# A two-layer streaming encoder step: where the MLP products' operands lie modulo 64 bytes, where sample combinations and first splits are kept, and another order in the MLP's opening

## The chip, the core and the metric

One core of a Trainium2 chip runs the whole step as one program. The metric is the device time of one execution in microseconds (us), median of several. Of the core's engines TensorE (PE) multiplies matrices, VectorE (DVE) and ScalarE (ACT) work elementwise, GpSimd (POOL) adds a little and issues some DMA, and SyncE (SP) issues most DMA.

## The reference

Two layers over a prompt of 1024 rows and 8 x 16 = 128 sample rows of width 1024. Layer 0 mixes by stick-breaking attention and a convolution module, layer 1 by banded attention. Both have the same MLP, which is what the change touches:

```
for layer in range(2):
    ...                                   # mixer and its output projection
    xp = xp + sq_relu_mlp(rmsnorm(xp, norm_ffn[layer]), w_up[layer], w_down[layer])
    xs = xs + sq_relu_mlp(rmsnorm(xs, norm_ffn[layer]), w_up[layer], w_down[layer])

def sq_relu_mlp(h, w_up, w_down):         # w_up 1024 x 4096, w_down 4096 x 1024, float32
    return jnp.square(jax.nn.relu(h @ w_up)) @ w_down
```

## The kernel before

**Products.** Each float32 operand is split in a rounded high part and a low remainder, and a product of two operands is three products on TensorE (high x high, high x low, low x high: `SPLIT`). The function `split` makes the high part on ScalarE (L186) and the low one on VectorE (L187). Both MLP matrices are multiplied in blocks by a scheme of seven products in place of eight (as Strassen's), so that sums of blocks of the activations and of the weights are made first.

**`rest(layer, ...)`** does, for one layer, the second half of the output projection (PSUM tiles `psob`), then the MLP's up stage, then its down stage. Its tiles in SBUF come from a pool under a name each (`own`: xr, xr2, xr3, hl0, hl1, th, tm, sm, lo0 to lo2, t1, sl0 to sl11); tiles named b11m, t2m, rwm, wm, wkm, hdm and the like come from another pool (`place`); weights in flight from a third (`sp`, names st for raw ones, hl_m and hl_wd for split ones). Pools are laid out one behind another in the order of first use.

**Up stage.** The blocks of the normed activations are `b11, b21, b22` and the sums `t1` to `t4`, each in four slices c, made by `combine` between the last products of the output projection (`evac`). `homes_of` and `where` say which tile each one lies in: t1, b21 and t3 of slice 2 are tiles lo0, lo1 and lo2, slices 0 and 1 are tiles sl. `units(u)`, u from 0 to 7, makes the hidden rows of one eighth of w_up: for k from 0 to 6 and two halves e, `seven(i, e)` with i = 7u + k prepares split weights, `mms` issues 12 products of 128 x 512 into `um` (L1604; moving operand: activations, stationary: weights) and `take` collects. The 128 sample rows take part by `sample(k)`, after products 0, 2, 3 and 6: its products `usm` (L1616) have the sample columns of a combination as stationary operand and the weights as moving one. A row `um<-t2m,hl_m` reads moving operand, then stationary. Those columns lie in the 128 last places (`NS`) of the tile of some combination, and `sample_combo` says of which. In unit 0 four pairs (k, e) are issued first over three slices (`early`), while the norms of the rows are still being finished (`ms_m`, `v_m`, by `rstd_of`).

**Down stage.** Products `pd` (L1889; activations moving, weights stationary) and, for the samples, `ps` (L1909; weights moving). `load_b` loads hidden blocks from HBM into the halves of xr, `split_b` splits them into four tiles in turn; `load_w` and `resident` load raw weights (a22 into lo0, lo1, lo2, xr3, sl8 to sl11, two blocks a tile; others into st), `weights_hi` makes their high part into hl_wd, hl0 or hl1 (L1830), `weights_lo` the low one (L1836). `run_at(i)` issues what is planned ahead of product i; `begin` issues the first two steps of it inside the last unit (u = 7) of the up stage.

**Order.** A scheduler orders each engine's instructions by expected times and by who waits for whom; what passes through `pinned` keeps the order in which it is written, and a tile is written anew only when all that read its last content are done.

Of the kernel before, what the change touches and what calls it, by code (L numbers as in the profile page):

```python
# [15 lines left out]
P = 128  # L16
# [108 lines left out]
def tile_trunk(ctx, tc, ins, outs):  # L125
# [132 lines left out]
    def rstd_of(r, pl, acc, scale, eps, name, pin=lambda ins: ins, cnt=NG):  # L258

        tp = P
        ms = bank(f"ms_{name}")
        for j in range(cnt):
            ins = mm(ms[:tp, j:j + 1], acc[:, j * tp:(j + 1) * tp], ones[:, 0:1], start=True, stop=True)
            if j == 0:
                pin(ins)
        v = pl.tile([P, 2, 4], F32, tag="rv", name=f"v_{name}")
# [1073 lines left out]
    def rest(layer, ks, cat, rst, mp, then, soon=None):  # L1342
# [12 lines left out]
        def pair(t, n=1024):  # L1355

            return t[:, :n].rearrange("p (a t) -> p a t", a=2)
# [29 lines left out]

        def sample_combo(key, c):

            return [home(k, c)[:, NS] for k in {"s1": ("b11", "t2"), "s2": ("b21", "b22"), "sd": ("t1", "t3")}[key]]  # L1390


        wo = ins["w_out_ab"] if layer == 0 else ins["w_out_c"]
# [50 lines left out]
        def evac(n, ps, g):  # L1444
            fc = order[n]
            xs = x[fc][:, g * G:g * G + G]
            tt(xs, xs, ps[:, :G], ALU.add)
            nx.square(xs, fc, slice(g * G, g * G + G), n == 0, add=nc.gpsimd.tensor_tensor)
            if g == NG - 1:
                put(xr_d[layer][fc], x[fc])  # L1450
                if n % 2:
                    todo.extend(combine(fc - 4))

                    if n < 7:
                        todo.append((lambda: (old(n + 3), old(n + 4))) if n < 4 else (lambda: whole_raw(0)))
            some(3)
            if n == KC - 1 and g == 1:
                seven(0, 0)


        raws, ups = {}, {}
# [27 lines left out]
        def seven(i, e):  # L1489
# [2 lines left out]
            m = 2 * u + e  # L1492
            if (i, e) in ups or m >= NF // 2:
                return
            a11, a12, a21, a22 = (raws[m, r][:, h * 512:h * 512 + 512] for r in range(2) for h in range(2))
            if k == 0:
                src = a11
            elif k == 1:
                if ("s1", m) not in ups:
                    two_sums(m)  # L1500
# [92 lines left out]
        def units(u):  # L1593
# [68 lines left out]
            start = 0  # L1662
            if u == 0:

                early = ((0, 0), (1, 0), (2, 0), (0, 1))
                for n, (k, e) in enumerate(early):
                    mms(k, e, range(3))
                    if n == 0:
                        seven(2, 0)
                    elif n == 1:  # L1670
                        seven(0, 1)
                    some(4)
                some(99)
                nx.end(0, pin=pinned)
# [115 lines left out]
        def split_b(i):  # L1790
            while len(bsplit) < 4 and len(bsplit) <= i:
                q = len(bsplit)
                if q < 2:
                    bsplit.append(pair(own(("th", "xr2")[q], F32R)))
# [412 lines left out]
```

## Time and profile before

| | us |
|---|---|
| median of 3 runs (lowest, highest) | 2742.29 (2740.29, 2743.49) |
| the profiled execution's own time | 2734.41 |
| its span in the trace | 2732.6 |
| up stage of layer 0, from first um to first pd | 577.00 to 956.46 |
| up stage of layer 1 | 1981.16 to 2354.97 |

All times in the profile are from the one profiled execution, counted from the span's start; 1.8 us lie around the span. A row of the timeline reads: start, length, engine, line, operation, out<-in by the program's names with buffer numbers left out (the second input of a product is the stationary one), partitions x elements, and how many instructions follow one another in it; in brackets, how long the engine stood idle before it and whose result ended that. Windows give the engines' busy time in a stretch, then the mean granted TensorE clock (1.00 is full), the busy share of the DMA engines and their rate.

### The profile page before, as it was taken

How to read it: one execution, taken by the hardware profiler on the slowest of the kernel's cores; microseconds unless marked ns; L12 is line 12 of the kernel's file. 1: busy time of each engine (PE TensorE's matmuls, PEld its weight loads, DVE VectorE, ACT ScalarE, POOL GpSimd, SP SyncE). 2: the span in 40 equal slices, each digit the busy share in tenths (PEclk: the TensorE clock that was granted, in tenths of full speed). 3: DMA queues.
4: the chain of work that ended last, by engine and by line, in shares of the span. 5: the costliest groups of instructions: out<-in, count | busy, mean ns of one | idle time of the engine just before them, and what ended most of it. 6: DMA issues, size and time to landing. Idle time of an engine off the chain costs nothing.

```text
span 2732.6 us, 42141 instructions
## 1 busy us (share of the span) xinstructions
PE 2672.6 (98%) x15404; PEld 2317.0 (85%) x15404; DVE 1988.5 (73%) x3820; ACT 1342.6 (49%) x2691; POOL 314.8 (12%) x535
## 2 busy tenths in 40 slices
PE   8999999999999999999999999999999999999998
PEld 8898877888888778888999999989978888788888
DVE  8999987886766644767577777778886767546677
ACT  6344457754444443445355555556554544433444
POOL 1000110121111100000011111110311111000001
PEclk9999999999999999999999999999999999999999
DMA  4444556533444387435544444446533434685344
GB/s 158 117 122 146 155 169 217 185 104 142 147 151 145 130 311 245 143 115 179 158 139 138 141 138 136 140 149 221 182 129 139 151 143 146 244 274 167 98 145 141
DMA packets 193807, 437.04 MB, mean 160 GB/s; under 512 B 26960, under 2 KB 71184, under 8 KB 191552
## 3 DMA queue, kind: packets, MB, share of 16 engines
q1 hardware_dynamic: 154032, 297.69, 33.5%
q0 software_dynamic: 39424, 136.64, 14.3%
q8 instruction: 121, 1.98, 0.3%
q14 instruction: 86, 0.70, 0.1%
q10 hardware_dynamic: 144, 0.02, 0.0%
HBM read 299.03 MB, written 122.58 MB: 154 GB/s over the span
## 4 chain that ended last, share of the span: by engine, by line
PE 83%; DVE 9%; ACT 3%; DMA 3%; issue 2%; POOL 0%; SPq 0%; DVEq 0%; ACTq 0%; POOLq 0%
PE um L1604 22%; PE psc L226 10%; PE psp L226 4%; PE usm L1616 3%; PE ps L1909 3%; PE psoa L226 2%; PE avc L488 2%; PE tpc L476 2%; PE f L226 1%; PE pd100None L1889 1%; PE pd000None L1889 1%; PE pd001None L1889 1%; PE pd101None L1889 1%; PE pd002None L1889 1%; PE pd102None L1889 1%
## 5 line engine op out<-in xcount | busy, mean ns | idle before, releaser
L226 PE MATMUL psc<-h,hl_wc 128*128 128x384 f32 x1728 | 329.1, 340 | 0.0
L226 PEld LDWEIGHTS psc<-h,hl_wc 128*128 128x128 f32 x1728 | 296.9, 188 | 9.2 <-issue 7.9
L1604 PE MATMUL um<-sl,hl_m 128*128 128x512 f32 x780 | 201.9, 398 | 0.0
L756 DVE SCALAR_TENSOR_TENSOR y<-u,dw,y 128x1024 f32<-128x1024 f32 (+1 forms) x232 | 177.4, 805 | 0.7
L1604 PEld LDWEIGHTS um<-sl,hl_m 128*128 128x128 f32 x780 | 145.2, 188 | 34.3
L226 PE MATMUL psp<-h,hl_wi 128*128 128x384 f32 x864 | 162.4, 340 | 0.0
L226 PEld LDWEIGHTS psp<-h,hl_wi 128*128 128x128 f32 x864 | 148.3, 188 | 6.2 <-issue 5.1
L187 DVE TENSOR_TENSOR tm<-xr,tm 128x512 fp32r<-128x512 f32 (+1 forms) x120 | 78.2, 652 | 101.6 <-ACT tm L186 101.4
L186 ACT ACTIVATE tm<-xr 128x512 fp32r<-128x512 f32 (+1 forms) x120 | 71.9, 599 | 124.0 <-PE pd103None L1889 26.1
L1230 ACT ACTIVATE s<-s,mxc 128x640 f32<-128x640 f32 (+4 forms) x128 | 88.8, 694 | 40.4 <-DVE mxc L1227 38.7
L186 ACT ACTIVATE whc<-tpc 128x512 fp32r<-128x512 f32 (+1 forms) x144 | 72.2, 523 | 63.8 <-PE tpc L476 60.6
L1227 DVE CUSTOM_DVE_ANT_0 s<-zc,bp 128x384 f32<-128x384 f32 (+3 forms) x128 | 66.0, 517 | 41.3 <-PE zc L1264 40.8
L1604 PE MATMUL um<-sl,hl 128*128 128x512 f32 x372 | 94.2, 392 | 0.5 <-DVE hl L187 0.5
L187 DVE TENSOR_TENSOR xr<-xr,xr 128x512 fp32r<-128x512 f32 (+1 forms) x60 | 39.2, 654 | 75.5 <-ACT xr L186 75.2
L187 DVE TENSOR_TENSOR wlc<-tpc,whc 128x512 fp32r<-128x512 f32 (+1 forms) x144 | 83.1, 594 | 7.5 <-ACT whc L186 6.7
L1628 ACT ACTIVATE xr<-xr 128x512 f32<-128x512 f32 x64 | 40.4, 632 | 91.4 <-DVE xr L1627 91.4
L1604 PEld LDWEIGHTS um<-sl,hl 128*128 128x128 f32 x372 | 69.0, 188 | 16.1 <-DVE hl L187 1.4
L1604 PE MATMUL um<-b11m,hl_m 128*128 128x512 f32 x288 | 72.5, 404 | 6.3 <-ACT hl_m L186 5.5
L476 PE MATMUL tpc<-ident,s 128*128 128x128 f32 x480 | 73.5, 276 | 3.6 <-DVE s L1232 3.0
L187 DVE TENSOR_TENSOR th<-xr,th 128x512 fp32r<-128x512 f32 (+1 forms) x62 | 40.6, 655 | 49.3 <-ACT th L186 49.3
L186 ACT ACTIVATE hl_m<-xr 128x512 fp32r<-128x512 f32 x54 | 34.1, 631 | 78.4 <-PE usm L1616 64.4
L1604 PEld LDWEIGHTS um<-b11m,hl_m 128*128 128x128 f32 x288 | 54.8, 195 | 18.8 <-ACT hl_m L186 6.4
(1055 smaller groups left out, 7150.8 us busy)
## 6 DMA issues: line engine op xcount, KB each, us to landing
xr<-hb_d SPq DMA_DIRECT2D x208, 256.0 KB, 2.8
xr<-in_w_up_dram SPq DMA_DIRECT2D x32, 512.0 KB, 3.8
rwm<-in_w_up_dram SPq DMA_DIRECT2D x32, 512.0 KB, 4.8
hb_d<-xr POOLq DMA_DIRECT2D x32, 512.0 KB, 3.3
hb_d<-t POOLq DMA_DIRECT2D x32, 512.0 KB, 3.2
wm<-in_w_down_dram SPq DMA_DIRECT2D x64, 256.0 KB, 3.5
st_wd<-in_w_down_dram SPq DMA_DIRECT2D x64, 256.0 KB, 3.5
st_wc<-in_w_in_c_dram SPq DMA_DIRECT2D x44, 256.0 KB, 2.9
```

Source lines behind the costliest of these rows:

```text
L186: ACT(hi, src, AF.Copy)
L187: return tt(lo, src, f(hi), ALU.subtract)
L226: mm(ps()[:, :G], hl[:, a, at:at + P], act[g][k // 4][b][:, k % 4, :], start=n == 0, stop=n == len(todo) - 1)
L476: nc.tensor.transpose(tp[:, c0 + q * P:c0 + (q + 1) * P], blocks.get(j, tile_q), ident)
L488: mm(st["av"][:, o0:o0 + n], vs[:, j, i].rearrange("p a d -> p (a d)"), src[:, c0:c0 + n], start=st["done"] == 0, stop=st["done"] == nmm - 1)
L756: stt(src if j == CW - 1 else dst, src, wj, dst, ALU.mult, ALU.add)
L1227: nc.vector.tensor_tensor_reduce(s[:, c:c + m], z, b, -1.0, mx, ALU.add, ALU.min, new)
L1230: ACT(s[:, :n], s[:, :n], AF.Exp, bias=mx, scale=-1.0, accum_out=tot)
L1604: mm(banks[b, e], w[a][:, c], combo(key, c)[:, h], start=k < 3 and c == 0 and i == 0, stop=c == 3 and i == 2, skip_group_check=k > 2)
L1616: mm(samples[u][:, e * 256:e * 256 + 256], sample_combo(key, c)[h], w[a][:, c].rearrange("p e t -> p (e t)"), start=k == 0 and c == 0 and ...
L1889: mm(ps, w[:, a, m * P:m * P + P], b[:, h], start=first and s == 0, stop=j == NJ - 1 and s == 2, skip_group_check=k not in heads)
L1909: mm(rows[e], s[:, h], w[:, a], start=j == 0 and q == 0 and k != 0, stop=j == NJ - 1 and q == 2 and k != 3, skip_group_check=k in (3, 0))
```

## The change

Five edits, the kernel otherwise as before:

1. In `rstd_of` the tile v is [P, 2, 8] in place of [P, 2, 4], 64 bytes a partition in place of 32. What is laid out behind it moves by 32 bytes.
2. `sample_combo`: the sample columns of s1 lie in the tiles of t1 and t2 (before b11 and t2), s2 in b21 and t3 (before b21 and b22), sd in t4 and b22 (before t1 and t3). Sample products k = 0 and 2 use s1, 3 uses s2, 6 uses sd.
3. `split_b`: the first two of the four tiles for split blocks are the halves of tm, the other two th and xr2 (before the other way round).
4. seven(0, 1) is called right behind seven(0, 0), at the end of the output projection; its block a11 comes from a tile st_a11 of its own, by one more load of 256 KB in each layer, in place of raws[1].
5. `early`: (0,0), (0,1), (1,0), (2,0) in place of (0,0), (1,0), (2,0), (0,1).

Two lines are added above the MLP's lines, so L1604 is L1606 after, L1616 is L1618, L1581 is L1583; the down stage's lines keep their numbers.

```
--- before.py
+++ after.py
@@ -265,7 +265,7 @@
             ins = mm(ms[:tp, j:j + 1], acc[:, j * tp:(j + 1) * tp], ones[:, 0:1], start=True, stop=True)
             if j == 0:
                 pin(ins)
-        v = pl.tile([P, 2, 4], F32, tag="rv", name=f"v_{name}")
+        v = pl.tile([P, 2, 8], F32, tag="rv", name=f"v_{name}")
         m, y = v[:, 0, :cnt], v[:, 1, :cnt]
         nc.vector.tensor_scalar(m, ms[:tp, 0:cnt], scale, eps, ALU.mult, ALU.add)
         ACT(y, m, AF.Sqrt)
@@ -1387,7 +1387,7 @@
 
         def sample_combo(key, c):
 
-            return [home(k, c)[:, NS] for k in {"s1": ("b11", "t2"), "s2": ("b21", "b22"), "sd": ("t1", "t3")}[key]]
+            return [home(k, c)[:, NS] for k in {"s1": ("t1", "t2"), "s2": ("b21", "t3"), "sd": ("t4", "b22")}[key]]
 
 
         wo = ins["w_out_ab"] if layer == 0 else ins["w_out_c"]
@@ -1456,6 +1456,7 @@
             some(3)
             if n == KC - 1 and g == 1:
                 seven(0, 0)
+                seven(0, 1)
 
 
         raws, ups = {}, {}
@@ -1492,9 +1493,10 @@
             m = 2 * u + e
             if (i, e) in ups or m >= NF // 2:
                 return
-            a11, a12, a21, a22 = (raws[m, r][:, h * 512:h * 512 + 512] for r in range(2) for h in range(2))
+            if i or not e:
+                a11, a12, a21, a22 = (raws[m, r][:, h * 512:h * 512 + 512] for r in range(2) for h in range(2))
             if k == 0:
-                src = a11
+                src = a11 if i or not e else staging(ins["w_up"][layer, 2][:, :512], f"a11{name}")
             elif k == 1:
                 if ("s1", m) not in ups:
                     two_sums(m)
@@ -1662,13 +1664,11 @@
             start = 0
             if u == 0:
 
-                early = ((0, 0), (1, 0), (2, 0), (0, 1))
+                early = ((0, 0), (0, 1), (1, 0), (2, 0))
                 for n, (k, e) in enumerate(early):
                     mms(k, e, range(3))
                     if n == 0:
                         seven(2, 0)
-                    elif n == 1:
-                        seven(0, 1)
                     some(4)
                 some(99)
                 nx.end(0, pin=pinned)
@@ -1790,8 +1790,8 @@
         def split_b(i):
             while len(bsplit) < 4 and len(bsplit) <= i:
                 q = len(bsplit)
-                if q < 2:
-                    bsplit.append(pair(own(("th", "xr2")[q], F32R)))
+                if q > 1:
+                    bsplit.append(pair(own(("th", "xr2")[q - 2], F32R)))
                 else:
                     bsplit.extend(pair(temp_again()[:, h:h + 1024]) for h in (0, 1024))
             n = bs[i].shape[1]
```

The places of the two operands modulo 64 bytes, by the addresses in the two built programs (moving, stationary; number of products):

| products | before | after |
|---|---|---|
| um L1604, 128 x 512 | (0,0) 468, (32,32) 828, (0,32) 972, (32,0) 420 | (32,32) 2688 |
| pd L1889, 128 x 512 | (0,0) 912, (0,32) 1584 | (32,32) 2496 |
| pd L1889, 128 x 256 | (0,32) 384 | (32,32) 384 |
| ps L1909, 128 x 512 | (0,0) 132, (32,0) 252 | (32,32) 384 |
| usm L1616, 128 x 256 | mixed | (32,32) 768 |
| psob, 128 x 384, of L226 | (32,0) 360, else (32,32) | (32,32) |

Before, the tiles of `own` lie at 0 (xr, xr2, xr3, th, tm, sm, hl0, hl1, lo, sl, t1) and those of `place` and of the stream pool at 32 (b11m, t2m, hl_m, hl_wd, st, rwm, wm, wkm, hdm); after, all lie at 32.

TensorE at the opening of layer 0's up stage; the four digits of um are the layer, u, the bank that a product adds to and e (um0020 collects product 2 of unit 0, e = 0). Before:

```order
L1604 MATMUL um0000_6306<-b11m0_20_6138,hl_m000_6244 128x512 x2
L1604 MATMUL um0000_6306<-b11m0_20_6138,hl_m001_6245 128x512
L1604 MATMUL um0010_6328<-t2m0_01_5842,th0_5634 128x512 x3
L1604 MATMUL um0010_6328<-t2m0_11_6007,th0_5634 128x512 x3
L1604 MATMUL um0010_6328<-t2m0_21_6162,th0_5634 128x512 x3
L1604 MATMUL um0020_6350<-sl00_5645,hl00_5632 128x512 x2
L1604 MATMUL um0020_6350<-sl00_5645,hl10_5633 128x512
L1604 MATMUL um0020_6350<-sl10_5646,hl00_5632 128x512 x2
L1604 MATMUL um0020_6350<-sl10_5646,hl10_5633 128x512
L1604 MATMUL um0020_6350<-lo00_5637,hl00_5632 128x512 x2
L1604 MATMUL um0020_6350<-lo00_5637,hl10_5633 128x512
L1604 MATMUL um0001_6368<-b11m0_00_5808,hl_m000_6244 128x512 x2
```

After:

```order
L1606 MATMUL um0000_6310<-b11m0_20_6138,hl_m000_6244 128x512 x2
L1606 MATMUL um0000_6310<-b11m0_20_6138,hl_m001_6245 128x512
L1606 MATMUL um0001_6332<-b11m0_00_5808,hl_m000_6244 128x512 x2
L1606 MATMUL um0001_6332<-b11m0_00_5808,hl_m001_6245 128x512
L1606 MATMUL um0001_6332<-b11m0_10_5973,hl_m000_6244 128x512 x2
L1606 MATMUL um0001_6332<-b11m0_10_5973,hl_m001_6245 128x512
L1606 MATMUL um0001_6332<-b11m0_20_6138,hl_m000_6244 128x512 x2
L1606 MATMUL um0001_6332<-b11m0_20_6138,hl_m001_6245 128x512
L1606 MATMUL um0010_6352<-t2m0_01_5842,th0_5634 128x512 x3
L1606 MATMUL um0010_6352<-t2m0_11_6007,th0_5634 128x512 x3
L1606 MATMUL um0010_6352<-t2m0_21_6162,th0_5634 128x512 x3
L1606 MATMUL um0020_6370<-sl00_5645,hl00_5632 128x512 x2
```

um0001, the second half of product 0, stands behind um0000 in place of standing behind um0020. Both need only b11m; um0001's weights hl_m000 and hl_m001 are those that seven(0, 1) makes as the other half of the same tiles.

ScalarE around the last sample products of layer 0 (usm07). Before:

```order
L1628 ACTIVATE xr20_5630<-xr20_5630 128x512
L1629 ACTIVATE xr20_5630<-xr20_5630 128x512
L1573 ACTIVATE sl00_9079<-usm07_8770,v_m02_6411 128x512
L186 ACTIVATE th0_9024<-xr0_8964 128x512
L1628 ACTIVATE hdm0_51_6424<-hdm0_51_6424 128x512
L1629 ACTIVATE hdm0_51_6424<-hdm0_51_6424 128x512
L1830 ACTIVATE hl_wd00_9018<-lo00_8968 128x512
L1628 ACTIVATE hdm0_51_6424<-hdm0_51_6424 128x512
L1830 ACTIVATE hl_wd01_9020<-lo00_8968 128x512
L1830 ACTIVATE hl_wd02_9022<-lo10_8971 128x512
L186 ACTIVATE xr20_9027<-xr0_8964 128x512
```

After:

```order
L1630 ACTIVATE xr20_5630<-xr20_5630 128x512
L1631 ACTIVATE xr20_5630<-xr20_5630 128x512
L1830 ACTIVATE hl_wd00_9020<-lo00_8970 128x512
L1830 ACTIVATE hl_wd01_9022<-lo00_8970 128x512
L1830 ACTIVATE hl00_5632<-lo20_9017 128x512
L1630 ACTIVATE xr20_5630<-xr20_5630 128x512
L1631 ACTIVATE xr20_5630<-xr20_5630 128x512
L1830 ACTIVATE hl_wd02_9024<-lo10_8973 128x512
L1575 ACTIVATE sl00_9079<-usm07_8772,v_m02_6413 128x512
L1830 ACTIVATE hl_wd03_9086<-lo10_8973 128x512
L186 ACTIVATE th0_9088<-xr0_8966 128x512
```

The splits of the first down weights (hl_wd00 and hl_wd01 from lo00, hl00 from lo20, hl_wd02 from lo10) stand ahead of sl00<-usm07 in place of behind it; so do the first splits of hidden blocks, tm0, some rows further up, in place of th0<-xr0.

TensorE at the passage from layer 0's up stage to its down stage (pd06m is product 6, bank m). Before:

```order
L1616 MATMUL usm07_8770<-hl_m0551_8926,t1m0_40_6322 128x256
L1889 MATMUL pd060None_9091<-th0_9024,hl_wd00_9018 128x512 x2
L1889 MATMUL pd061None_9095<-th0_9024,hl_wd00_9018 128x512 x2
L1889 MATMUL pd062None_9099<-th0_9024,hl_wd00_9018 128x512 x2
L1889 MATMUL pd063None_9103<-th0_9024,hl_wd00_9018 128x512 x2
L1909 MATMUL ps06_9107<-hl_wd00_9018,sm0_5636 128x512 x2
L1581 MATMUL utm07_9143<-ident_69,sl00_9079 128x128 x4
L1889 MATMUL pd060None_9091<-th0_9024,hl_wd00_9018 128x512
L1889 MATMUL pd061None_9095<-th0_9024,hl_wd00_9018 128x512
L1889 MATMUL pd062None_9099<-th0_9024,hl_wd00_9018 128x512
L1889 MATMUL pd063None_9103<-th0_9024,hl_wd00_9018 128x512
```

After:

```order
L1618 MATMUL usm07_8772<-hl_m0551_8928,t4m0_71_6349 128x256
L1889 MATMUL pd060None_9092<-tm0_8976,hl_wd00_9020 128x512
L1889 MATMUL pd061None_9096<-tm0_8976,hl_wd00_9020 128x512
L1889 MATMUL pd062None_9100<-tm0_8976,hl_wd00_9020 128x512
L1889 MATMUL pd063None_9104<-tm0_8976,hl_wd00_9020 128x512
L1889 MATMUL pd060None_9092<-tm0_8976,hl_wd00_9020 128x512
L1889 MATMUL pd061None_9096<-tm0_8976,hl_wd00_9020 128x512
L1889 MATMUL pd062None_9100<-tm0_8976,hl_wd00_9020 128x512
L1889 MATMUL pd063None_9104<-tm0_8976,hl_wd00_9020 128x512
L1909 MATMUL ps06_9108<-hl_wd00_9020,sm0_5636 128x512
L1889 MATMUL pd060None_9092<-tm0_8976,hl_wd00_9020 128x512
L1889 MATMUL pd061None_9096<-tm0_8976,hl_wd00_9020 128x512
```

The last sample product reads t4m in place of t1m and t3m; the four small transposes utm07 move some ten products back, and the products of the first step read tm0 in place of th0.

SP at the end of the output projection, with the added load. Before, then after:

```order
L1403 DMA xr0_5629<-xm_d0_112 128x1152 x2
L193 DMA st_wo0b6_1_5983<-in_w_out_ab_dram 128x512
L193 DMA st_wo0b7_0_6066<-in_w_out_ab_dram 128x128
L193 DMA st_wo0b7_1_6070<-in_w_out_ab_dram 128x512
L1403 DMA xr20_5630<-xm_d0_112 128x1152
L1403 DMA xr30_5631<-xm_d0_112 128x1152
L1471 DMA xr0_5629<-in_w_up_dram 128x1024 x2
```

```order
L1403 DMA xr0_5629<-xm_d0_112 128x1152 x2
L193 DMA st_wo0b6_1_5983<-in_w_out_ab_dram 128x512
L193 DMA st_wo0b7_0_6066<-in_w_out_ab_dram 128x128
L193 DMA st_wo0b7_1_6070<-in_w_out_ab_dram 128x512
L193 DMA st_a11m0_6248<-in_w_up_dram 128x512
L1403 DMA xr20_5630<-xm_d0_112 128x1152
L1403 DMA xr30_5631<-xm_d0_112 128x1152
L1472 DMA xr0_5629<-in_w_up_dram 128x1024 x2
```

One row is added, st_a11m, behind the last weights of the output projection and ahead of the loads into xr2 and xr3.

More of the change, by code (lines that the diff above doesn't have):

```diff
@@ L267, in rstd_of @@
                 pin(ins)
-        v = pl.tile([P, 2, 4], F32, tag="rv", name=f"v_{name}")
+        v = pl.tile([P, 2, 8], F32, tag="rv", name=f"v_{name}")
         m, y = v[:, 0, :cnt], v[:, 1, :cnt]
@@ L1388, in sample_combo @@
         def sample_combo(key, c):
-            return [home(k, c)[:, NS] for k in {"s1": ("b11", "t2"), "s2": ("b21", "b22"), "sd": ("t1", "t3")}[key]]
+            return [home(k, c)[:, NS] for k in {"s1": ("t1", "t2"), "s2": ("b21", "t3"), "sd": ("t4", "b22")}[key]]
         wo = ins["w_out_ab"] if layer == 0 else ins["w_out_c"]
@@ L1458, in evac @@
                 seven(0, 0)
+                seven(0, 1)
         raws, ups = {}, {}
@@ L1494, in seven @@
                 return
-            a11, a12, a21, a22 = (raws[m, r][:, h * 512:h * 512 + 512] for r in range(2) for h in range(2))
+            if i or not e:
+                a11, a12, a21, a22 = (raws[m, r][:, h * 512:h * 512 + 512] for r in range(2) for h in range(2))
             if k == 0:
-                src = a11
+                src = a11 if i or not e else staging(ins["w_up"][layer, 2][:, :512], f"a11{name}")
             elif k == 1:
@@ L1669, in units @@
                         seven(2, 0)
-                    elif n == 1:
-                        seven(0, 1)
                     some(4)
@@ L1792, in split_b @@
                 q = len(bsplit)
-                if q < 2:
-                    bsplit.append(pair(own(("th", "xr2")[q], F32R)))
+                if q > 1:
+                    bsplit.append(pair(own(("th", "xr2")[q - 2], F32R)))
                 else:
```

2 lines of the change are left out of this document (1 added, 1 removed).

## Prediction

> **What bounds the kernel now.** I read the page's busy shares first, then the chain that ended last, then the work by stretches of the span, then TensorE's rows at the places the change touches.
>
> ```profile
> span 2732.6 us, 42141 instructions
> PE 2672.6 (98%) x15404; PEld 2317.0 (85%) x15404; DVE 1988.5 (73%) x3820; ACT 1342.6 (49%) x2691; POOL 314.8 (12%) x535
> PE 83%; DVE 9%; ACT 3%; DMA 3%; issue 2%; POOL 0%; SPq 0%; DVEq 0%; ACTq 0%; POOLq 0%
> ...
> core 0: us, PE busy (x) PEld busy (x) DVE busy (x) ACT busy (x) POOL busy (x), PEclk, DMA share, GB/s
> 660.00:930.00 270.00, 270.00 (x1321) 226.17 (x1320) 187.29 (x282) 126.49 (x216) 37.21 (x54) 1.00 0.41 146
> 960.00:1320.00 360.00, 358.94 (x1566) 292.08 (x1567) 230.16 (x386) 159.44 (x278) 15.10 (x28) 1.00 0.60 196
> ```
>
> The first row gives the span, the second shows TensorE busy for 98% of it, the third that 83% of the chain that ended last is its products. The last two rows are stretches inside layer 0's up stage and down stage: TensorE is busy for all of 270.00 us and for 358.94 of 360.00, at the full granted clock. There, whatever shortens a product shortens the kernel, and no other engine's work can. What is left to gain otherwise lies in a few places where the products wait: the opening of each up stage and the passage from up to down stage.
>
> **Part 1, the places modulo 64 bytes.** A product's records overlap, so I take the time from the start of one row to the start of the next, over its count. The table of places in the section on the change says which pairs of operands are alike.
>
> ```profile
> 682.04 5.77 PE L1604 MATMUL um<-b11m,hl 128*128 128x512 f32 x24
> 687.65 0.28 PE L1616 MATMUL usm<-hl,b11m 128*128 128x256 f32 x1
> ...
> 727.13 5.61 PE L1604 MATMUL um<-b11m,hl_m 128*128 128x512 f32 x24
> 732.59 0.28 PE L1616 MATMUL usm<-hl_m,b11m 128*128 128x256 f32 x1
> ...
> 734.38 5.72 PE L1604 MATMUL um<-t2m,hl_m 128*128 128x512 f32 x24
> 739.93 1.56 PE L1604 MATMUL um<-sl,hl 128*128 128x512 f32 x6
> ...
> 1133.29 0.86 PE L1889 MATMUL pd000None<-tm,hl_wd 128*128 128x512 f32 x3
> 1138.89 0.86 PE L1889 MATMUL pd000None<-th,hl 128*128 128x512 f32 x3
> ...
> 1140.97 0.84 PE L1889 MATMUL pd003None<-th,hl 128*128 128x512 f32 x3
> 1143.69 0.85 PE L1889 MATMUL pd003None<-xr,hl 128*128 128x512 f32 x3
> ```
>
> In the up stage, b11m with hl (unlike) takes (687.65 - 682.04) / 24 = 233.8 ns a product; b11m with hl_m (alike) 5.46 / 24 = 227.5; t2m with hl_m (alike too) 5.55 / 24 = 231.3. In the down stage eight rows of three from 1133.29 to 1138.89 (tm with hl_wd, unlike) take 5.60 / 24 = 233.3, four rows from 1140.97 to 1143.69 (th and xr with hl, alike) 2.72 / 12 = 226.7. So an unlike pair costs 2.5 to 6.6 ns more, with TensorE always busy and at full clock; the same b11m is fast and slow, so it is the pair and not the tile.
>
> After the change all pairs of the MLPs are alike. By the table, 1392 products of L1604, 1584 of L1889 with 512 columns, and 252 of L1909 stop being unlike. For L1889 I take the 6.6 ns just shown: 1584 x 6.6 ns = 10.5 us. L1909 is the same form with the operands exchanged; at 6.6 ns it is 252 x 6.6 = 1.7 us. For L1604 the alike rows spread from 227.5 to 231.3; with every pair alike I expect 228.5, nearer the low end, because a group with hl_m at 231.3 stands between groups that are unlike and the down stage's alike rows lie at 226.7: 1392 x (234.0 - 228.5) = 7.7 us, with 234.0 the rounded unlike value. Sum 19.9, say 20 us.
>
> Bounds. Low: 2.5 ns for L1604 (3.5 us), 10.5 for L1889, nothing for L1909, 14 us. High: all L1604 products at 227.5, which also speeds up those alike already (1392 x 6.3 = 8.8 us and at most 1296 x 3.8 = 4.9 us), 26 us. For the 768 sample products and the 384 of 256 columns in the down stage I take nothing; the upper bound, half of 6.6 ns for half the columns, would add 1152 x 3.3 ns = 3.8 us. The 32 bytes themselves (v's tile) add no instruction.
>
> A rule speaks against this part. The Trainium skill, "TensorE: Matmul & The Clock Gate", section "Step-by-step: what each phase is for", says that TensorE reads the moving operand and the next weights through two independent ports, so that a weight load takes nothing from the running product. By it the places would be worth nothing; the rows above differ by pair and disagree. I keep what follows from it as rival A.
>
> **Part 2, from up to down stage.** The order's excerpts show it: before, layer 0's first down product waits for hl_wd00, made on ScalarE from lo00, and the load into lo00 waits until the last sample products (L1616) have read lo00.
>
> ```profile
> 935.59 1.28 SPq L1732 DMA_DIRECT2D xr<-hb_d  x3
> 952.11 2.34 SPq L1732 DMA_DIRECT2D lo<-in_w_down_dram  x4
> ...
> 955.78 0.63 ACT L1830 ACTIVATE hl_wd<-lo 128x512 fp32r<-128x512 f32 x1 [0.93 <-DMA lo<-in_w_down_dram]
> ...
> 952.15 0.28 PE L1616 MATMUL usm<-hl_m,t1m 128*128 128x256 f32 x1
> 956.46 1.22 PE L1889 MATMUL pd060None<-th,hl_wd 128*128 128x512 f32 x2 [4.03 <-ACT hl_wd L1830]
> ...
> 960.74 0.74 PE L1909 MATMUL ps<-hl_wd,sm 128*128 128x512 f32 x2 [0.81 <-DMA sm<-hs_d]
> ...
> 962.24 0.51 PE L1889 MATMUL pd060None<-th,hl_wd 128*128 128x512 f32 x1 [0.32 <-DVE hl_wd L1836]
> ...
> 2350.18 0.28 PE L1616 MATMUL usm<-hl_m,t1m 128*128 128x256 f32 x1
> 2354.97 0.82 PE L1889 MATMUL pd160None<-th,hl_wd 128*128 128x512 f32 x2 [4.51 <-ACT hl_wd L1830]
> ...
> 2359.48 0.50 PE L1889 MATMUL pd160None<-th,hl_wd 128*128 128x512 f32 x1
> ...
> 952.40:960.80 8.40, 3.56 (x10) 2.52 (x9) 2.40 (x4) 5.33 (x10) 0.84 (x2) 0.80 0.92 319
> ```
>
> From the last sample product to the first product with a low part are 962.24 - 952.15 = 10.09 us in layer 0 and 2359.48 - 2350.18 = 9.30 in layer 1. The work in it is one sample product (0.12), ten products (2.34) and four small transposes (0.36): 2.82 us. So 7.3 and 6.5 us are lost, 13.8 in all, part of it to the clock, whose mean in layer 0 is 0.80 over these 8.40 us.
>
> After the change the lo tiles are read last by sample products of 2 and 4, some 14 us earlier. SP's four loads can then be issued right behind the three at 935.59, and tm takes the first b-split, which stood on th before and had to wait for it. By the two rows, a load issued at 952.11 gives its first split at 955.78, 3.7 us on; issued at about 937 it is done near 941, 11 us before it is wanted. SP's queue has nothing else in it that waits. What is late next: the third PSUM bank (pd062), freed by ScalarE's sl<-usm, and VectorE's low parts. I leave 0.3 to 1.5 us a layer for these and take 0.9: a gain of 13.8 - 1.8 = 12 us. Ends: 8 (the wait for sm or for a low part of about 3 us stays in each layer) and 13.8.
>
> **Part 3, the opening.** seven(0,1) is called a step earlier, from a block loaded apart, and its products come right after those of seven(0,0).
>
> ```profile
> 577.00 2.24 PE L1604 MATMUL um<-b11m,hl_m 128*128 128x512 f32 x9
> ...
> 587.92 4.70 PE L1604 MATMUL um<-b11m,hl_m 128*128 128x512 f32 x9 [2.76 <-ACT hl_m L186]
> ...
> 604.78 2.47 PE L1604 MATMUL um<-t2m,hl_m 128*128 128x512 f32 x10
> ...
> 1981.16 2.24 PE L1604 MATMUL um<-b11m,hl_m 128*128 128x512 f32 x9
> ...
> 1991.15 0.73 PE L1604 MATMUL um<-b11m,hl_m 128*128 128x512 f32 x2 [2.76 <-ACT hl_m L186]
> 1992.50 1.89 PE L1604 MATMUL um<-b11m,hl_m 128*128 128x512 f32 x7 [0.61 <-DVE hl_m L187]
> ...
> 2002.73 2.56 PE L1604 MATMUL um<-t2m,hl_m 128*128 128x512 f32 x10
> ...
> 577.00:588.00 11.00, 7.31 (x29) 4.74 (x28) 10.73 (x17) 7.71 (x15) 4.90 (x5) 0.97 0.55 204
> 588.00:601.00 13.00, 12.87 (x39) 10.41 (x40) 7.37 (x19) 4.37 (x9) 0.00 (x0) 0.50 0.00 0
> ```
>
> The second b11m row waits 2.76 us for hl_m, and behind it layer 0 runs 13 us at half clock: from the stage's first product to t2m,hl_m are 27.8 us in layer 0 and 21.6 in layer 1. The 6.2 us between them are the half clock, since 39 records in 13.00 us are 6.5 us of work at full clock.
>
> The change takes this wait away: the high and low parts of hl_m for seven(0,1) are there before, and nine products more stand ahead of t2m,th. But VectorE is busy for 10.73 of these 11.00 us with combinations and splits that the change does not reduce, and hl_m010, wanted next, comes behind them and behind the row norms (v_m) in its order. So most of the wait moves to t2m,hl_m010, some 14 us into the stage. Layer 1 shows what can be gained at full clock: 2.76 + 0.61 = 3.4 us at most. Following each engine's order with the durations before, I get t2m,hl_m010 there about 2.5 us late, and so take 0.9 us a layer. Layer 0 gains the half clock's 6.2 besides, if the new wait does not bring it back. A wait of 2.76 us brought it in layer 0 and not in layer 1, so I take about six chances in ten that it stays away: 0.9 + 0.9 + 6.2 x 0.6 = 5.5 us. Ends: 6 us lost (half clock in layer 1 as well, no gain in layer 0) and 9 gained. The Trainium skill has this clock too (same page, "What's actually happening"): an idle window of about 3.4 us that runs freely halves it, so where the wait falls decides; that one of two like waits did it agrees.
>
> The added load is 256 KB in each layer, ahead of others on SP's queue.
>
> ```profile
> xr<-hb_d SPq DMA_DIRECT2D x208, 256.0 KB, 2.8
> ...
> wm<-in_w_down_dram SPq DMA_DIRECT2D x64, 256.0 KB, 3.5
> ...
> 956.00:1024.00 68.00, 66.41 (x283) 53.41 (x284) 32.70 (x55) 28.27 (x48) 2.57 (x4) 0.97 0.89 313
> 548.00:577.00 29.00, 29.00 (x168) 29.00 (x167) 26.17 (x41) 16.85 (x34) 14.11 (x14) 1.00 0.41 139
> ```
>
> The last row is the stretch in which it is issued, behind st_wo's: the DMA engines are busy for 0.41 of it. By the rows above it a load of this size lands in 2.8 to 3.5 us. I take nothing; at most 3.5 us a layer, if the raw weights behind it arrive that much later.
>
> **The sum.** 20 + 12 + 5.5 = 37.5 us less than the profiled execution, 2734.4 us (span 2732.6 and 1.8 around it): 2696.9. That execution stands 7.9 us under the median of the runs, 2742.3; on the median it is 2704.8, so 2705.
>
> **Rivals.** A: the places cost nothing, and the 4 to 7 ns come from something else that goes with the pairs (which group stands before, which tile another engine is reading). For it speaks the port rule and the spread of alike rows; against it b11m, fast and slow with different weights only. Then 2742.3 - 17.5 = 2725. B: the wait only moves. In both openings the clock halves behind t2m,hl_m010 (6 us lost instead of 5.5 gained), or the passage keeps 4 us; 2742.3 - 20 - 12 + 6 = 2716, or 2709. For it speaks VectorE's 10.73 of 11.00 us. C, on the other side: all tiles now lie 32 bytes off, those that DMA fills among them, and a transfer to such a place takes longer. xr<-hb_d goes from 0 to 32, and wm, at 32 already, takes 3.5 us against its 2.8. In the first 68 us of layer 0's down stage the DMA engines are busy for 0.89, and I take layer 1's as like it; at 3.5 / 2.8 = 1.25 they would need 1.11 of the time, 7.6 us lost a layer, and the kernel still gains 22 (2720). It becomes slower than before by 0.2% (5.5 us) only if a layer loses (37.5 + 5.5) / 2 = 21.5 us there, transfers 1.48 times as long: 68 x (0.89 x 1.48 - 1) = 21.6. Against it: wm reads weights and xr activations, so their difference needs no place to explain it. D: the change does not do what it says, because the shift moves other operands to unlike places; the table has none left.
>
> **The numbers.** The forecast with its own range of 2697 to 2712 has 0.60, B 0.20, A 0.10, C with 1.25 and smaller sizes 0.05, C at 1.48 or A together with B 0.05. A measurement of this kernel tells 0.2%, 5.5 us, from no change. Only the last case can come near zero: faster 0.94, within 0.2% 0.03, slower 0.03. The range takes in B, A and the high end of part 1 with little else: 2694 to 2726.
>
> **What would show it.** Right: rows of L1604 (then L1606) and L1889 all 226 to 230 ns apart whatever the weights; the lo loads issued by 940 and no wait over 1 us at pd060 and pd160; um0001 directly behind um0000 without a wait, one wait of 1 to 4 us at t2m,hl_m010, the clock at 1.00 in layer 0's opening. Wrong: pairs still 233 apart (A); half clock behind the new wait (B); longer transfers into xr and TensorE waiting on SP's loads in the first 68 us of the down stages (C).

## The result and the profile after

| kernel | median (lowest, highest), us | ratio to before, 95% interval |
|---|---|---|
| before | 2741.63 (2740.29, 2743.49) | |
| changed | 2719.43 (2714.57, 2725.46) | 0.992 (0.9897 to 0.9942) |

The changed kernel is 22 us faster, between 16 and 28 by the interval. The forecast was 2705, 14 us lower. The forecast's own range of 2697 to 2712 does not hold the time; the outer range (2694 to 2726), opened to take in rivals A and B, does. Its profiled execution took 2717.19 us.

The page after, first rows:

```profile
span 2715.4 us, 42145 instructions
PE 2665.4 (98%) x15404; PEld 2314.9 (85%) x15404; DVE 1989.4 (73%) x3820; ACT 1343.6 (49%) x2691; POOL 316.4 (12%) x535
```

TensorE still fills 98% of the span with the same 15404 records. The span is 17.2 us shorter (from 2732.6): TensorE's busy time fell by 7.2 us of these (from 2672.6), and the other 10 are idle time that is gone.

Rows of TensorE's timeline after, for the pairs that the prediction showed:

```profile
678.32 5.66 PE L1606 MATMUL um<-b11m,hl 128*128 128x512 f32 x24
683.83 0.28 PE L1618 MATMUL usm<-hl,sl 128*128 128x256 f32 x1
...
730.49 5.71 PE L1606 MATMUL um<-t2m,hl_m 128*128 128x512 f32 x24
...
1122.13 0.86 PE L1889 MATMUL pd000None<-th,hl_wd 128*128 128x512 f32 x3
1127.73 0.85 PE L1889 MATMUL pd000None<-tm,hl 128*128 128x512 f32 x3
...
1130.48 0.84 PE L1889 MATMUL pd000None<-tm,hl 128*128 128x512 f32 x3
1133.20 0.86 PE L1889 MATMUL pd000None<-th,hl_wd 128*128 128x512 f32 x3
```

Here part 1 fails. th and xr with hl_wd take (1127.73 - 1122.13) / 24 = 233.3 ns a product, as the pairs with hl_wd did before, though both operands now lie at 32 modulo 64; tm with hl takes (1133.20 - 1130.48) / 12 = 226.7, as the pairs with hl did before. Of the pairs shown only b11m with hl became quicker, (683.83 - 678.32) / 24 = 229.6 in place of 233.8. From b11m,hl to the second t2m,hl_m behind it, the same number of products of each width in both kernels, are 52.34 us before (682.04 to 734.38) and 52.17 after.

The passage from up to down stage, SP, ScalarE and TensorE, layer 0 and then layer 1:

```profile
932.49 2.57 SPq L1732 DMA_DIRECT2D lo<-in_w_down_dram  x4
...
940.89 1.14 ACT L1830 ACTIVATE hl_wd<-lo 128x512 fp32r<-128x512 f32 x2
...
947.71 0.28 PE L1618 MATMUL usm<-hl_m,t4m 128*128 128x256 f32 x1
947.83 0.39 PE L1889 MATMUL pd060None<-tm,hl_wd 128*128 128x512 f32 x1
...
957.01 0.50 PE L1889 MATMUL pd060None<-th,hl_wd 128*128 128x512 f32 x1 [0.66 <-DVE th L187]
...
2340.15 0.28 PE L1618 MATMUL usm<-hl_m,t4m 128*128 128x256 f32 x1
2340.27 0.39 PE L1889 MATMUL pd160None<-tm,hl_wd 128*128 128x512 f32 x1
```

The loads are issued at 932.49, before the last sample products, the first split is made at 940.89, and the first down product starts 0.12 us behind the last sample product in both layers, where 4.03 and 4.51 us of idle time stood. One wait for a low part of th is left in each layer, 0.66 us in layer 0 and 0.72 in layer 1.

The opening:

```profile
580.16 4.28 PE L1606 MATMUL um<-b11m,hl_m 128*128 128x512 f32 x18
...
598.40 0.73 PE L1606 MATMUL um<-t2m,hl_m 128*128 128x512 f32 x2 [2.39 <-ACT hl_m L186]
...
604.75 0.28 PE L1618 MATMUL usm<-hl,sl 128*128 128x256 f32 x1
...
1972.32 4.28 PE L1606 MATMUL um<-b11m,hl_m 128*128 128x512 f32 x18
...
1989.96 1.02 PE L1606 MATMUL um<-t2m,hl_m 128*128 128x512 f32 x2 [2.40 <-ACT hl_m L186]
...
1997.17 0.28 PE L1618 MATMUL usm<-hl,sl 128*128 128x256 f32 x1
...
588.00:602.00 14.00, 10.44 (x58) 8.15 (x57) 13.99 (x44) 9.25 (x19) 1.10 (x1) 1.00 0.10 42
1990.20:1993.60 3.40, 3.40 (x9) 2.62 (x9) 3.40 (x11) 2.27 (x5) 0.00 (x0) 0.50 0.00 0
```

The wait did move: 2.39 and 2.40 us for hl_m at t2m, with VectorE busy for 13.99 of 14.00 us. The clock stayed at 1.00 in layer 0 and was halved for 3.40 us in layer 1, which it was not before. From the first um to the first sample product of product 2 are 604.75 - 580.16 = 24.6 us in layer 0 and 24.9 in layer 1.

### The profile page after: what moved, and what is told of

Same layout as the page of the kernel before. It is cut to its first block, busy times and chain, and to the rows that moved or that the text cites. A ratio compares the mean times of both kernels' runs of the same rounds, so it can differ in the third digit from the quotient of the medians.

```text
span 2715.4 us, 42145 instructions
## 1 busy us (share of the span) xinstructions
PE 2665.4 (98%) x15404; PEld 2314.9 (85%) x15404; DVE 1989.4 (73%) x3820; ACT 1343.6 (49%) x2691; POOL 316.4 (12%) x535
## 4 chain that ended last, share of the span: by engine, by line
PE 84%; DVE 9%; ACT 3%; DMA 2%; issue 2%; SPq 0%; DVEq 0%; ACTq 0%
PE um L1606 22%; PE psc L226 10%; PE psp L226 4%; PE usm L1618 3%; PE ps L1909 3%; PE psoa L226 3%; PE avc L488 2%; PE tpc L476 2%; PE f L226 1%; PE zs L589 1%; PE pd100None L1889 1%; PE pd000None L1889 1%; PE pd102None L1889 1%; PE pd002None L1889 1%; PE pd101None L1889 1%
## 5 line engine op out<-in xcount | busy, mean ns | idle before, releaser
L226 PE MATMUL psc<-h,hl_wc 128*128 128x384 f32 x1728 | 329.1, 340 | 0.0
L226 PEld LDWEIGHTS psc<-h,hl_wc 128*128 128x128 f32 x1728 | 297.0, 188 | 9.2 <-issue 7.9
L1606 PE MATMUL um<-sl,hl_m 128*128 128x512 f32 x780 | 201.3, 397 | 0.0
L1606 PEld LDWEIGHTS um<-sl,hl_m 128*128 128x128 f32 x780 | 144.8, 188 | 34.1
L226 PE MATMUL psp<-h,hl_wi 128*128 128x384 f32 x864 | 162.5, 340 | 0.0
L226 PEld LDWEIGHTS psp<-h,hl_wi 128*128 128x128 f32 x864 | 148.3, 188 | 6.2 <-issue 5.1
L1606 PE MATMUL um<-sl,hl 128*128 128x512 f32 x372 | 95.5, 396 | 0.0
L1606 PEld LDWEIGHTS um<-sl,hl 128*128 128x128 f32 x372 | 69.7, 189 | 15.8
L186 ACT ACTIVATE th<-xr 128x512 fp32r<-128x512 f32 (+1 forms) x62 | 37.3, 601 | 66.4 <-PE pd103None L1889 14.1
L1263 PE MATMUL zc<-k,q 128*128 128x384 f32 (+1 forms) x192 | 66.1, 345 | 2.4 <-DVE cpc L498 2.4
```

The costliest lines, as they stand in the source:

```text
L186: ACT(hi, src, AF.Copy)
L226: mm(ps()[:, :G], hl[:, a, at:at + P], act[g][k // 4][b][:, k % 4, :], start=n == 0, stop=n == len(todo) - 1)
L1263: mm(z[:, :m], qs[i][:, qc], kd[i][:, kc], start=True, stop=False)
L1606: mm(banks[b, e], w[a][:, c], combo(key, c)[:, h], start=k < 3 and c == 0 and i == 0, stop=c == 3 and i == 2, skip_group_check=k > 2)
```

## The experiments

Gains below are against the kernel before on the same chip, where its median was 2739.7 to 2740.2 us. Theory 64 is the prediction's; theory 128 is what I put in its place after seeing the trace, where the pairs that stayed slow lie 64 bytes apart modulo 128.

**Places apart from the rest.** places32_alone is the kernel before with v of [P, 2, 8] alone, others_alone the changed kernel with [P, 2, 4]. The two others take [P, 2, 16], which puts every MLP operand at 96 modulo 128:

```
-        v = pl.tile([P, 2, 4], F32, tag="rv", name=f"v_{name}")
+        v = pl.tile([P, 2, 8], F32, tag="rv", name=f"v_{name}")      # places32_alone
+        v = pl.tile([P, 2, 16], F32, tag="rv", name=f"v_{name}")     # before_all128, after_all128
```

> The kernel before with v of [P, 2, 8] alone: the tiles of own move from 64 to 32 modulo 128, those of place and of the stream pool stay at 96, so all MLP pairs are alike modulo 64, and the 3228 products that were unlike are 64 apart modulo 128. Theory 128 (a product is quick when its moving operand and the next weights lie alike modulo 128 bytes, and 32 or 64 apart costs the same): products that were at 233 to 234 ns stay at 233, gain 0 to 3 us, 2739 to 2742. Theory 64 (the prediction's): 14 to 26 us, 2716 to 2728.

> The changed kernel with v back at [P, 2, 4]: places as before, the passage and the opening as changed. Theory 128: within 3 us of the changed kernel, 2717 to 2724, since the places gave nothing. Theory 64 with a smaller gain in the passage and opening: slower than the changed kernel by 14 us or more, above 2733.

> The changed kernel with v of [P, 2, 16]: the tiles of own move to 96 modulo 128, so that every moving operand and every weight tile of the MLPs lies at 96 modulo 128. Theory 128: all pitches fall to 227 to 228 ns; 5568 products of 512 columns, now 231.1 on average, save 3.5 ns each: 18 to 22 us, 2697 to 2702. Theory pools (the difference goes with the two operands being in certain pools, or with distance, not with the address modulo anything): no change from the changed kernel, 2717 to 2722.

> The kernel before with v of [P, 2, 16] and nothing else: all MLP pairs alike modulo 128. Theory 128: 18 to 24 us faster than before, 2718 to 2724. Theory pools: 2740 to 2743.

| kernel | median, us | ratio, 95% interval |
|---|---|---|
| places32_alone | 2736.65 | 0.9991 (0.9981 to 1.0001) |
| others_alone | 2720.79 | 0.9930 (0.9917 to 0.9943) |
| after_all128 | 2716.68 | 0.9916 (0.9903 to 0.9929) |
| before_all128 | 2734.67 | 0.9984 (0.9975 to 0.9993) |

The shift by itself is worth 2.5 us (0 to 5), which can't be told from nothing; the other edits give 19 (16 to 23). Theory 64 is out. Theory 128 falls too: with all pairs alike modulo 128 the times hardly move. So either places mean nothing, or the period is longer than 128.

**The pair by itself.** A kernel that fills one tile over nearly all of SBUF and times groups of 96 products at chosen addresses (cut to its core):

```
w, x = at(wb), at(xb)
for k in range(8):
    for m in range(4):
        for i, (a, h) in enumerate(SPLIT):
            mm(banks[m], w[:, a, m * P:m * P + P], x[:, h], ...)
```

> The disputed cost by itself: no step of the model is computed; one tile over nearly all of SBUF is filled, and groups of 96 products of 128 x 512 (three a bank, four banks, as in the down stage) run with the two operands at chosen byte addresses. Weights at 87904 (lower half of SBUF, as hl_wd) and at 132192 (upper half, as hl0), moving operand at 13 addresses from 8032 to 204896, all at 96 modulo 128; then shifts of 16, 32 and 64 bytes; then four groups with ScalarE and VectorE splitting beside them. Theory halves (a pair is quick, 227 ns, when both operands lie in the same half of SBUF, and 232 to 234 across): weights at 87904 quick with the moving operand below about 114688 and slow above it, weights at 132192 the other way round; shifts change it by 2 ns at most. Theory modulo: all 26 groups of the scan at 227, the shifted ones at 233. Theory traffic (the difference comes from what ScalarE, VectorE and the DMA queues do beside the products): all groups without traffic alike at 227, and only the last four differ.

Its timeline, a row a group (l: weights at 87904, u: at 132192, the second letter the moving operand's address; ma, mb, mc: weights at 87904 and the moving operand moved by 16, 32 and 64 bytes):

```profile
39.05 21.92 PE L159 MATMUL la<-z 128*128 128x512 f32 x96
60.81 21.92 PE L159 MATMUL lb<-z 128*128 128x512 f32 x96
...
604.81 22.40 PE L159 MATMUL ma<-z 128*128 128x512 f32 x96
627.05 22.57 PE L159 MATMUL mb<-z 128*128 128x512 f32 x96
649.46 22.14 PE L159 MATMUL mc<-z 128*128 128x512 f32 x96
```

Each of the 26 groups of the scan takes (604.81 - 39.05) / 26 = 21.76 us from start to start, 226.7 ns a product, wherever the two tiles lie; 32 bytes more make it (649.46 - 627.05) / 96 = 233.4. From 600 to 820 us VectorE, ScalarE and the DMA engines are busy for 0.00 us, so the slow pace needs no traffic: halves are out and places matter. The last four groups, which were to have splits beside them, do not test traffic. Nothing held the splits back, and they ran from 29.14 to 73.60 us, beside la and lb, which kept 21.76 us; DMA beside the products was not tried in this kernel.

The 13 moving addresses were all apart from the weights by multiples of 256, which I had not noticed in choosing them. Some of them are 256 apart modulo 512 (le is) and as quick as those at 0; and the kernels with all operands at 96 modulo 128, which hardly moved, have 3228 of the MLPs' 5568 products of 512 columns 128 or 384 apart modulo 512. Together this points to a period of 256; I still tried it against 512.

**The curve, and the kernels by it.** The same micro-kernel with the distance as variable, and both kernels with a tile of 416 bytes ahead of own's tiles (the changed one with v back at [P, 2, 4]), which makes all distances in the MLPs multiples of 512:

```
     rst = Bufs(ctx.enter_context(pool("rstd")), rv=3)
+    pad = ctx.enter_context(tc.tile_pool(name="pad", bufs=1)).tile([P, 104], F32, name="pad")
+    nc.gpsimd.memset(pad, 0.0)
```

> The disputed cost by itself once more, now as a curve: no step of the model is computed; groups of 96 products as in the first such run, weights at 87904, moving operand at 149856 plus 0 to 480 bytes, for 512 columns, then both operands shifted together, then 384 and 256 columns. In the first run all 26 quick groups were apart by multiples of 256 bytes, and shifts of 32 gave 233.3, of 64 228.9 ns. Theory 512 (what counts is the distance modulo 512 bytes): 0 gives 226.7, 192 and 320, the distances in the changed kernel, 233, and 128 and 384, those of the version with all at 96 modulo 128, 231 to 233; both shifted together stays at 226.7. Theory 256: as 512, but 256 gives 226.7 as well, and 192 equals 448. Theory traffic (the real kernels' slow pairs have another cause than place): 128, 192, 320 and 384 all at 227 to 229. For 384 and 256 columns I expect less than 1 ns.

> The changed kernel with v back at [P, 2, 4] and a tile of 416 bytes laid out ahead of the tiles of own, so that all MLP pairs are apart by multiples of 512 bytes. Theory 512: every pitch falls to 227; 5568 products at 231.1 on average now save 4.2 ns each, 23 us, so 2694 to 2700. Theory traffic: as the changed kernel, 2717 to 2722.

> The kernel before with the same tile of 416 bytes and nothing else. Theory 512: 5568 products at 231.6 on average save 4.7 ns each, 26 us, 2712 to 2718. Theory traffic: 2738 to 2742.

The timeline of the curve (da to dp: distances 0, 4, 8, 16, 32, 48, 64, 96, 128, 160, 192, 256, 320, 384, 416, 448; wa: both operands moved by 32):

```profile
45.98 21.92 PE L156 MATMUL da<-z 128*128 128x512 f32 x96
67.74 23.02 PE L156 MATMUL db<-z 128*128 128x512 f32 x96
90.60 22.56 PE L156 MATMUL dc<-z 128*128 128x512 f32 x96
...
179.73 22.15 PE L156 MATMUL dg<-z 128*128 128x512 f32 x96
201.72 22.56 PE L156 MATMUL dh<-z 128*128 128x512 f32 x96
224.12 22.56 PE L156 MATMUL di<-z 128*128 128x512 f32 x96
...
269.00 22.55 PE L156 MATMUL dk<-z 128*128 128x512 f32 x96
291.39 21.96 PE L156 MATMUL dl<-z 128*128 128x512 f32 x96
313.19 22.15 PE L156 MATMUL dm<-z 128*128 128x512 f32 x96
335.18 22.48 PE L156 MATMUL dn<-z 128*128 128x512 f32 x96
357.49 22.65 PE L156 MATMUL do<-z 128*128 128x512 f32 x96
379.98 22.56 PE L156 MATMUL dp<-z 128*128 128x512 f32 x96
...
424.77 21.93 PE L156 MATMUL wa<-z 128*128 128x512 f32 x96
446.55 21.95 PE L156 MATMUL wb<-z 128*128 128x512 f32 x96
```

| distance modulo 512 | 0 | 4 | 64 | 96 | 192 | 256 | 320 | 384 | 416 |
|---|---|---|---|---|---|---|---|---|---|
| ns a product, start to start | 226.7 | 238.1 | 229.1 | 233.3 | 233.2 | 227.1 | 229.1 | 232.4 | 234.3 |

Only the distance counts (both moved by 32 take (446.55 - 424.77) / 96 = 226.9), and its period is 256 within 0.8 ns: 256 is as quick as 0, 320 as 64, 384 (232.4) as 128 (233.2). Before, b11m,hl lies 416 apart by the program's addresses and sl,hl_m and th,hl_wd 96; after, 320 and 192. The curve says 234.3 to 229.1 for the first and 233.3 to 233.2 for the others: it gives what both traces show.

The same run also timed 384 and 256 columns, where I expected less than 1 ns, and that missed. At 384 columns distances 0, 32, 64 and 256 agree within 0.3 ns (173.3 to 173.6), but 128 costs 175.9. At 256 columns the order is another: 0 and 256 are the slowest with 119.8 ns, 32 and 64 take 117.8 to 117.9, and 192 is the quickest with 113.4.

| kernel | median, us | ratio, 95% interval |
|---|---|---|
| after_all512 | 2698.02 | 0.9849 (0.9835 to 0.9862) |
| before_all512 | 2715.77 | 0.9919 (0.9905 to 0.9932) |

after_all512, down stage and up stage:

```profile
1126.04 0.84 PE L1889 MATMUL pd000None<-th,hl_wd 128*128 128x512 f32 x3
...
1130.80 0.84 PE L1889 MATMUL pd003None<-xr,hl_wd 128*128 128x512 f32 x3
...
676.88 5.63 PE L1606 MATMUL um<-b11m,hl 128*128 128x512 f32 x24
...
728.50 5.71 PE L1606 MATMUL um<-t2m,hl_m 128*128 128x512 f32 x24
```

hl_wd's products stand (1130.80 - 1126.04) / 21 = 226.7 ns apart, and the sequence that took 52.17 us in the changed kernel takes 51.62. The kernel before gains 22 us by the tile alone (19 to 26). By the curve its products of 512 columns that lay 96 apart (972 of L1604, 1584 of L1889) save 6.6 ns each and those that lay 416 apart (420 of L1604, 252 of L1909) 7.6 ns, 22.0 us in all. The changed kernel with the tile and without the shift is at 2698, 41 us (38 to 45) under before: a version that beats both.

**Opening and passage apart**, each from the kernel before: the opening's edits (4 and 5 of the change); sample_combo's and split_b's together; each of these two alone.

> The kernel before with the other opening alone (seven(0,1) a step earlier from a block of its own, products in the new order), places as before. My reading of the two traces: the stretch from um0000 to the first row norms is 7.3 us shorter in layer 0 and 2 us in layer 1; of layer 0's, 6 hang on the half clock. 5 to 9 us faster, 2731 to 2735. Rival (the wait only moves): within 2 us of before.

> The kernel before with sample_combo's and split_b's edits alone. My reading of the two traces: 6.8 us in layer 0 and 5.9 in layer 1, so 12.7 us faster, 2726 to 2729. Rival (the loads come early, but another wait takes the place): 4 to 8 us.

> The kernel before with sample_combo's edit alone, split_b as before. The weights come early, but the first split of hidden rows still goes into th, which the last unit uses until about 953 us in layer 0. If the loads into lo are what was waited for, the products start some 1 to 2 us after the last sample product, and most of the 12.7 us stays: 9 to 12 us. If th is the next wait in line and as long: under 5 us.

> The kernel before with split_b's edit alone: the first split of hidden rows goes into tm, the loads into lo still wait for the last sample products. sample_combo's edit alone gave nothing and both together 11 us. Theory both needed (two waits of like length side by side, the weights' load and the tile for the first split): 0 to 2 us, 2737 to 2741. Rival (split_b's tile alone was the wait, the weights' load ends in its shadow): 8 to 11 us, 2729 to 2732.

| kernel | median, us | ratio, 95% interval |
|---|---|---|
| opening_alone | 2734.54 | 0.9980 (0.9970 to 0.9991) |
| passage_alone | 2728.89 | 0.9963 (0.9949 to 0.9977) |
| combo_alone | 2739.83 | 1.0000 (0.9989 to 1.0011) |
| splitb_alone | 2738.90 | 1.0001 (0.9991 to 1.0012) |

Opening 5.5 us (2.5 to 8), passage 10 us (6 to 14), and neither half of the passage anything. TensorE's and SP's rows of combo_alone, then of splitb_alone:

```profile
937.45 2.56 SPq L1732 DMA_DIRECT2D lo<-in_w_down_dram  x4
...
952.68 0.28 PE L1616 MATMUL usm<-hl_m,t4m 128*128 128x256 f32 x1
954.72 0.50 PE L1889 MATMUL pd060None<-th,hl_wd 128*128 128x512 f32 x1 [1.75 <-ACT th L186]
...
957.01 0.63 PE L1889 MATMUL pd061None<-th,hl_wd 128*128 128x512 f32 x1
957.44 0.63 PE L1889 MATMUL pd062None<-th,hl_wd 128*128 128x512 f32 x1
...
961.84 0.60 PE L1889 MATMUL pd060None<-th,hl_wd 128*128 128x512 f32 x1 [2.53 <-DVE hl_wd L1836]
```

```profile
949.99 2.34 SPq L1732 DMA_DIRECT2D lo<-in_w_down_dram  x4
...
954.31 0.73 PE L1889 MATMUL pd060None<-tm,hl_wd 128*128 128x512 f32 x2 [4.00 <-ACT hl_wd L1830]
```

With sample_combo alone the weights come early and th is late: 1.75 us for its high part, then 2.53 for a low part of hl_wd that VectorE makes only at 961.10, behind a low part of xr for which it had waited 1.38 us; the products between run at half clock (957.01 to 957.44, 0.43 us for one). With split_b alone tm is early and the weights are late, 4.00 us. Layer 1 shows the same in both runs (1.69 and 2.54 us; 4.50 us). Two conditions have to hold at once: with either one missing TensorE waits about as long as with both missing. That combo_alone gains nothing although its first idle time is 1.75 us in place of 4.03 goes against my 9 to 12 us.

## Why the prediction was right or wrong

**Part 1, the places: wrong.** 20 us were forecast, with 14 as the low end; the shift alone measured 2.5 (0 to 5). The step that failed is the table's key: "alike modulo 64". That pairs cost 226.7 or 233.3 ns by their places was right, and so was the price, which the micro-kernel reproduces; but the trace of before had only the distances 0 and 96 or 416 modulo 512 in it, and 64, 128, 256 and 512 as modulus sort these alike. I took the smallest, sized the gain as if the distance became 0, and it became 192 or 320. By the curve the shift is worth 3.5 us: 420 products of L1604 and 252 of L1909 go from 416 to 320, 5.2 ns each, and the other unlike ones from 96 to 192, which costs the same. Where the distance really becomes 0, the size of the forecast comes out: 22 us on the kernel before, and 22 between others_alone and after_all512 by their ratios. The bound should have had as its lower end no gain at all, since no row showed a pair 192 apart. One more reading was wrong: the 231.3 ns of t2m,hl_m, from which the spread of the alike rows was taken, do not come from its place. Its row takes 5.55 us before (734.38 to 739.93), and 5.55 in after_all512, where its distance is 0 as it was (728.50 to 734.05).

**Rival A** (the places cost nothing, 2725) stood at 0.10; its time is 6 us off, nearer than the forecast's. Its reason holds by half: something other than places modulo 64 goes with the pairs, and it is places modulo 256. B's 2716 is nearer still, but by luck: part 1 failed in its place.

**Part 2, the passage: right.** Forecast 12, measured alone 10 (6 to 14). The loads start 15 us ahead of the last sample product (932.49 to 947.71), and tm was needed as much: the runs of one half each show two waits side by side. The prediction named both and priced the stretch as a whole; only my expectation for combo_alone priced the loads alone. Left are 0.66 us in layer 0 and 0.72 in layer 1, of the 0.9 set aside in each; pd062's bank did not wait. A good part of the gain is the clock: in the five kept traces with both edits there is no half clock at the passage, and in the seven other traces of the whole kernel there are 3.4 to 10.2 us of it in layer 0 and 3.4 to 6.8 in layer 1.

**Part 3, the opening: right in size, in part by luck.** Forecast 5.5, measured alone 5.5 (2.5 to 8). From the stage's first product to the first sample product of product 2, layer 0 went from 31.3 us (577.00 to 608.26 before) to 24.6, layer 1 from 25.1 (1981.16 to 2006.29) to 24.9, with the half clock gone in one and come in the other: rival B held in layer 1 for 3.4 us of half clock. The wait at t2m,hl_m, forecast at about 2.5 us, is 2.4. But the one execution that the prediction read was not typical. In the seven kept traces with the old opening the same stretch takes 26.7 to 31.5 us in layer 0, 29.5 on average, and 25.1 to 30.9 in layer 1, 27.9 on average; in the five with the new one 25.2 and 24.7 on average. The old wait brought the half clock in layer 1 too, in every trace but before's, and with the new one it stays away in layer 0 in three of five and in layer 1 in one. So layer 1 gains more than the 0.9 us forecast, and layer 0 less than its trace alone showed.

**The sum.** Without part 1's error it is 2.5 + 12 + 5.5 = 20, against 22 measured. Rival C did not come: a load of 256 KB into xr lands in 2.8 us after as before, and in after_all512, where these tiles lie at 32 modulo 64 too, the kernel is the fastest of all. Rival D, that the change does not do what it says, was set aside by a table with the wrong modulus.

## What to carry to other kernels

When a trace shows two paces for the same instruction, list every distinct distance in it before naming the rule, and ask which untried distance the change will make; a micro-kernel with the distance as variable settles in one run what three shifted kernels do not. With products of 512 columns back to back, of the type float32r that these kernels give to split operands, lay out moving operands and weights so that they are multiples of 256 bytes apart, and measure this from the built addresses; for other widths measure the curve first, since at 256 columns it is another. Where two inputs are late together, removing one shows nothing; test them together before dropping an idea.

## What the runs showed of the hardware

A product of 128 x 512 takes 226.7 to 227.1 ns when its operands are 0 or 256 bytes apart modulo 512, 229 at 64 or 320, 233 to 234 at 32, 96, 128, 160 and 192, 238.1 at 4, at all the places in SBUF that the micro-kernels tried. The Trainium skill, "TensorE: Matmul & The Clock Gate", "Step-by-step: what each phase is for", has weight loads and moving reads on two independent ports; the micro-kernels disagree wherever the distance is no multiple of 256, and what conflicts there no run here shows.

The half clock comes in pieces of 3.41 us (four of them from 587.36 to 601.01 before, one from 1990.22 to 1993.63 after). How a wait is divided between two such pieces decides. These are the pieces ahead of the half clock before, in layer 0, of the one in layer 1 that brought none, and of the half clock after, in layer 1:

```profile
583.95:587.36 3.41, 1.21 (x6) 0.66 (x4) 3.41 (x6) 2.52 (x6) 1.86 (x2) 1.00 0.43 173
1986.83:1990.24 3.41, 1.56 (x7) 0.94 (x5) 3.41 (x6) 2.33 (x5) 1.87 (x2) 1.00 0.44 178
1986.81:1990.22 3.41, 1.01 (x8) 0.80 (x7) 3.40 (x19) 3.36 (x8) 0.00 (x0) 1.00 0.00 0
```

TensorE is idle in them for 2.20, 1.85 and 2.40 us, though the first two waits are alike with 2.76 us. In the openings of all twelve kept traces of the whole kernel a piece with 1.94 us or more of idle time was followed by half clock every time (19 pieces), and one with 1.85 or less never; elsewhere in these traces the border is less sharp. The half clock also comes where nothing was changed, in some executions and not in others:

```profile
51.50:54.90 3.40, 3.40 (x12) 3.40 (x11) 3.40 (x8) 1.57 (x3) 0.00 (x0) 0.50 0.00 0
112.90:116.30 3.40, 3.02 (x17) 1.99 (x17) 2.85 (x3) 1.74 (x5) 0.00 (x0) 0.50 0.00 0
```

The changed kernel's profiled execution has these two at its start, which before's has not, and reaches the up stage 3.2 us later (580.16 against 577.00). That accounts for 3 of the 5 us by which the profiled executions differ less (17) than the medians (22). That such pieces make the spread between runs of one kernel (3 and 11 us here) is in part borne out by the record: beside the experiments the kernel before took 2742.18 to 2748.92 us in its executions with a mean granted clock of 0.989 and 2734.49 to 2738.52 in those with 0.993, and 0.004 of 2740 us are 11. It is not all of it, since the changed kernel took 2717.19 and 2725.46 us at the same 0.993.
